# Block sums of w_out formed in DRAM instead of through SBUF, with two moves between queues and engines

## The chip, the cores and the metric

The kernel runs on one core of a Trainium2 chip. The metric is the device time of one execution in microseconds (us), lower is better. The core has five engines that the profile names PE (TensorE, the matrix engine; PEld is its weight load), DVE (VectorE), ACT (ScalarE), POOL (GpSimd) and SP (SyncE, which here only issues transfers). Transfers are issued from SP's, ACT's or POOL's instruction queue and are all carried by the same 16 DMA engines.

## The reference

One layer of an encoder on 512 frames of width 2048, all in float32. Cut to what matters here:

```
h = rmsnorm(x, g_pre);  proj = h @ w_in                # 2048 x 14368+
q, k, v -> conv(4), silu, l2norm;  o_a = gated delta rule, 16 heads, chunks of 64
y_a = (rmsnorm(o_a) * silu(z_a)) @ w_br_a
y_b = (silu(layernorm(conv31(glu(...)))) * silu(z_b)) @ w_br_b
mixed = (gate_a * y_a + gate_b * y_b) @ w_out
x = x + rmsnorm(mixed, g_post)
e = p @ w_ple_proj;  out = x + rmsnorm(sigmoid(x @ w_ple_gate) * e, g_ple)
```

## The kernel before

All large products run on PE as three float32r matmuls each: every operand is split into a high part (a cast on ACT) and a low part (a subtraction, on DVE or POOL), and high x high, high x low and low x high are added in PSUM. The time is a row of such products, one behind the other, and the other engines prepare the next pieces of weights while PE works.

**Start (`load_x`).** PE first makes the embedding `e = p @ w_ple_proj` (`embed`, 4 column tiles x 4 row tiles, 96 matmuls of 128x512). Each result goes from PSUM to an SBUF tile `e_sb` (L233, alternately ACT and DVE) and is stored to `pe_dram` (L309), to be read again at the end. Beside it the four row tiles of x are scaled by their inverse norm: `xss` (ACT and DVE), `xms` (DVE), `xrs` (a power on POOL, L265), then one half of x by DVE (L266) and one by ACT (L267). Then PE transposes x in 16 groups of four 128x128 blocks (`xp`, L313); of each group ACT makes the high part `hh` (L316) and DVE the low part `hl` (L317). The first product with `w_in` (L183, L185, L187: high x high, high weights x low, low weights x high) runs between the transposes. It walks over 16 k-blocks, 4 to a piece of weights. SP loads two pieces in one tile `raw` (L121, 512 KB, three buffers), ACT casts each (`w`, L126), DVE makes its low part (L127), and four `w` buffers stand ready. `hf` and `zsf` (L360) are sums of parts of h for a later stage.

**z, gates (to about 550 us).** A seven-product (Strassen-like) scheme with its block sums of weights on DVE.

**Heads (about 550 to 1490 us).** For 8 groups of two heads PE runs the q, k, v products, and `group` and `head_scan` do the delta rule between them: steps of these generators are taken after so many matmuls (`tick`). Within a group, POOL makes `nk` (L828) and scales `E` (L832); `W` is formed on DVE; its blocks are spread to `Ud` by four copies of 32 partitions x 1024 (L875, all on ACT); DVE transposes `Ud` into `UT` (L881) and solves a triangular system (L892, L893). At a group's end POOL makes `ors` (L786), on which DVE waits for the output of the heads (L790).

**presum.** The last but one product, `mixed @ w_out`, is a seven-product scheme as well. It wants four sums of blocks of w_out: T1 = B11+B12, T3 = B12+B22, T2 = T1+B22, T4 = T2+B21, each as 2 x 4 tiles of 128x1024. `presum` forms them while the heads run, on POOL's queue: blocks are loaded into SBUF tiles `wsum` (L1060, 256 KB), further blocks are added by the transfer itself (`accum_op=add`), and the sums are stored to `wo_sums` (L1065). Per (jp, q) these are 12 loads and 8 stores, 160 transfers in all. They are next read at 2081 us, by L1401.

**Order.** The program is written in one order, and a scheduler then lays each engine's instructions in a fixed order by its own model; `pin` (`keep_in_program_order`) holds instructions it is given. Each engine takes its instructions strictly in that order, so an instruction that waits holds up all behind it on its engine; a transfer waits in the queue of the engine that issues it.

The lines that the prediction speaks of: L309 (stores of the embedding), L265 to L267 (scaling of x), L313 to L317 (transposes), L121, L126, L127 (weights), L183 to L187 (the products), L875 and L881 (`Ud`, `UT`), L786, L828, L832, L847 (POOL's and DVE's steps in a group), L1060 and L1065 (presum).

Of the kernel before, what the change touches and what calls it, by code (L numbers as in the profile page):

```python
# [9 lines left out]
F32 = mybir.dt.float32  # L10
F32R = mybir.dt.float32r
AF = mybir.ActivationFunctionType
ALU = mybir.AluOpType
AX = mybir.AxisListType.X

P = 128
T = 512
# [64 lines left out]
def _body(ctx, tc, A, out):  # L82
    nc = tc.nc
# [7 lines left out]
    slots = ctx.enter_context(tc.tile_pool(name="slots", bufs=21, side="right"))  # L91
# [11 lines left out]
    pin = tc.keep_in_program_order  # L103
# [34 lines left out]
    jobs = deque()  # L138
    active = []

    def spawn(gen, period, key=None):
        active.append([gen, period, period, key])
# [51 lines left out]
    pe_dram = dram.tile([4, NTT, P, T], F32, name="pe_dram")  # L194
# [43 lines left out]
    def load_x():  # L238
        with tc.tile_pool(name="xin", bufs=1) as xin, tc.tile_pool(name="xps", bufs=6, space=PSUM) as xps:
# [66 lines left out]
            nc.sync.dma_start(cst[:, P:], A["consts"][:, P:])  # L306
            nc.sync.dma_start(vec[:, V_DW:], A["vecs"][:, V_DW:])
            for (j, tt), e in e_sb.items():
                nc.sync.dma_start(pe_dram[j, tt], e)  # L309
            for k in range(NK):  # L310
                ps = xps.tile([P, T], F32, tag="xp", name="xp")
                for tt in range(NTT):
# [30 lines left out]
    B11, B12, B22, B21 = range(4)  # L343
# [458 lines left out]
    def group(g):  # L802
# [7 lines left out]
        W = hd.tile([P, 8, 2, 64], F32, tag="W", name="W", bufs=1)  # L810
# [40 lines left out]
        for hh, h, s4, kq, kc, vc in heads:  # L851
            pg = wps.tile([P, NTT, 2, 64], F32, tag="w", name="pg")
            for c in range(8):
                tt, par = divmod(c, 2)
                a = 64 * par
# [12 lines left out]
        U = W[:, :, 0, :]  # L868
        QK = W[:, :, 1, :]

        Ud = hd.tile([P, 32, 4, 8], F32, tag="Ud", name="Ud", bufs=1)
        for qd in range(4):
            r = slice(32 * qd, 32 * qd + 32)
            b = 32 * (qd % 2)
            nc.scalar.copy(Ud[r], U[r, :, b:b + 32].rearrange("p x s -> p s x").unsqueeze(2).broadcast_to([32, 32, 4, 8]))  # L875
        yield
        VT = hd.tile([P, 32, 8], F32, tag="VT", name="VT", bufs=1)
        nc.gpsimd.tensor_copy(VT.rearrange("p j i -> p (j i)"), cc(C_VI, 256))
# [7 lines left out]
        for j in range(30, -1, -1):  # L886
            n, i0 = 32 - j, j // 4
# [161 lines left out]
    WO = A["w_out"]  # L1049
    T1, T2, T3, T4 = range(4)  # L1050
    sums = dram.tile([2, 4, 4, P, 1024], F32, name="wo_sums")
    def presum():
        for jp in range(2):
            for q in range(4):
                cs = [slice(n * T, n * T + T) for n in range(2)]
                a = [slots.tile([P, T], F32, tag="s", name="wsum") for n in range(2)]

                def take(t, blk, add):
                    for n in range(2):
                        nc.gpsimd.dma_start(t[n], WO[jp, blk, q][:, cs[n]], **(dict(accum_op=ALU.add) if add else {}))  # L1060
                        yield

                def give(t, m):
                    for n in range(2):
                        nc.gpsimd.dma_start(sums[jp, m, q][:, cs[n]], t[n])  # L1065
                        yield
                yield from take(a, B11, False)
                b = [slots.tile([P, T], F32, tag="s", name="wsum") for n in range(2)]
                yield from take(b, B12, False)
                yield from take(a, B12, True)  # L1070
                yield from take(b, B22, True)
                yield from give(a, T1)
                yield from give(b, T3)
                yield from take(a, B22, True)
                yield 24
                yield from give(a, T2)
                yield from take(a, B21, True)
                yield 24
                yield from give(a, T4)

    rest = deque([lambda i=i: zb_tile(i) for i in range(FILL, NK)] + [f for i in range(2) for f in (lambda i=i: glu_b(i), lambda i=i: glu_a(i))])
    for g in range(NH // 2):
        pair = (2 * g, 2 * g + 1)
        for h in pair:
            gemm_cm(w_in_tile(16 + h), hT, evac_k(h))
            gemm_cm(w_in_tile(h), hT, evac_q(h))
            gemm_cm(w_in_tile(32 + h), hT, evac_v(h))
        jobs.append(lambda g=g: spawn(group(g), HP, "heads"))
        if g == 0:
            jobs.append(lambda: spawn(presum(), 13, "presum"))  # L1090
        for _ in range(2):
            if rest:
                rest.popleft()()
# [667 lines left out]
```

## Time and profile before

| | |
|---|---|
| median of 3 runs | 2436.09 us (2435.22 to 2436.59) |
| the profiled execution: its own time | 2434.78 us |
| its span, first to last instruction | 2433.0 us |
| PE busy | 2411.8 us, 99% |
| DVE, ACT, POOL busy | 1783.4 (73%), 1210.6 (50%), 491.7 us (20%) |
| moved by DMA | 380 MB, mean 156 GB/s |

The profile has a page (busy time, the chain of waits that ended last, groups of instructions), and views of the trace behind it: who waited for whom, instructions in order of time, busy time by stretch, transfers. Busy time of PE counts matmuls that are pipelined, one beginning before the last has ended, so what PE loses is read as gaps in its order of time. An engine's idle time costs something only where PE stands still for it. The span is 1.8 us shorter than the execution's own time, the rest lying around the first and last instruction.

### The profile page before, as it was taken

How to read it: one execution, taken by the hardware profiler on the slowest of the kernel's cores; microseconds unless marked ns; L12 is line 12 of the kernel's file. 1: busy time of each engine (PE TensorE's matmuls, PEld its weight loads, DVE VectorE, ACT ScalarE, POOL GpSimd, SP SyncE). 2: the span in 40 equal slices, each digit the busy share in tenths (PEclk: the TensorE clock that was granted, in tenths of full speed). 3: DMA queues.
4: the chain of work that ended last, by engine and by line, in shares of the span. 5: the costliest groups of instructions: out<-in, count | busy, mean ns of one | idle time of the engine just before them, and what ended most of it. 6: DMA issues, size and time to landing. Idle time of an engine off the chain costs nothing.

```text
span 2433.0 us, 33728 instructions
## 1 busy us (share of the span) xinstructions
PE 2411.8 (99%) x11966; PEld 1983.7 (82%) x11966; DVE 1783.4 (73%) x3360; ACT 1210.6 (50%) x2355; POOL 491.7 (20%) x521
## 2 busy tenths in 40 slices
PE   9999999999999999999999999999999999999998
PEld 6888888887788888888888887888887888888886
DVE  8877888776677776767777668999988654667644
ACT  6455555555655555564555554454424433554532
POOL 0001110013213031232200001998840000000000
PEclk9999999999999999999999999999999999999999
DMA  7577676757546362657522222443444333665552
GB/s 269 162 200 204 192 208 206 211 155 211 155 140 175 99 187 88 177 149 202 165 89 99 82 80 73 156 139 104 157 133 160 131 130 100 231 223 165 194 175 76
DMA packets 145434, 380.21 MB, mean 156 GB/s; under 512 B 16369, under 2 KB 24817, under 8 KB 145265
## 3 DMA queue, kind: packets, MB, share of 16 engines
q1 hardware_dynamic: 119152, 319.32, 39.3%
q0 software_dynamic: 23808, 54.54, 10.3%
q10 hardware_dynamic: 2304, 4.20, 0.6%
q8 instruction: 94, 1.54, 0.3%
q14 instruction: 76, 0.61, 0.1%
HBM read 329.75 MB, written 48.23 MB: 155 GB/s over the span
## 4 chain that ended last, share of the span: by engine, by line
PE 93%; DVE 4%; ACT 1%; issue 1%; POOL 0%; DMA 0%; SPq 0%; DVEq 0%; POOLq 0%; ACTq 0%
PE g L185 14%; PE g L187 14%; PE g L183 14%; PE zp L473 6%; PE zp L474 6%; PE zp L475 6%; PE yp L1147 4%; PE yp L1145 4%; PE yp L1143 4%; PE f L1438 2%; PE f L1437 2%; PE f L1439 2%; PE f L1610 2%; PE f L1612 2%; PE f L1611 2%; PE psB L760 1%
## 5 line engine op out<-in xcount | busy, mean ns | idle before, releaser
L187 PE MATMUL g<-hh,w 128*128 128x512 f32 x1536 | 609.4, 397 | 3.0 <-DVE w L127 3.0
L185 PE MATMUL g<-hl,w 128*128 128x512 f32 x1536 | 610.4, 397 | 0.0
L183 PE MATMUL g<-hh,w 128*128 128x512 f32 x1536 | 608.5, 396 | 1.0 <-ACT w L126 1.0
L126 ACT CAST w<-raw 128x512 fp32r<-128x512 f32 x580 | 353.2, 618 | 445.6 <-PE g L187 179.6
L127 DVE TENSOR_TENSOR w<-raw,w 128x512 fp32r<-128x512 f32 x466 | 320.8, 695 | 182.0 <-ACT w L126 179.4
L187 PEld LDWEIGHTS g<-hh,w 128*128 128x128 f32 x1536 | 289.0, 188 | 59.8 <-DVE w L127 5.8
L183 PEld LDWEIGHTS g<-hh,w 128*128 128x128 f32 x1536 | 289.2, 188 | 55.5 <-ACT w L126 1.9
L185 PEld LDWEIGHTS g<-hl,w 128*128 128x128 f32 x1536 | 289.0, 188 | 55.5 <-issue 1.2
L1005 DVE SCALAR_TENSOR_TENSOR uc<-up,vec,uc 128x497 f32<-128x497 f32 (+29 forms) x390 | 282.2, 733 | 13.2 <-ACT uc L984 1.9
L127 POOL TENSOR_TENSOR w<-raw,w 128x512 fp32r<-128x512 f32 x114 | 146.9, 1304 | 59.6 <-ACT w L126 59.3
L707 DVE SCALAR_TENSOR_TENSOR cv<-g,vec,cv 128x511 f32<-128x511 f32 x144 | 106.3, 738 | 27.3 <-ACT cv L705 26.6
L1143 PE MATMUL yp<-w,uh 128*128 128x512 f32 x256 | 100.3, 393 | 0.1
L1145 PE MATMUL yp<-w,uh 128*128 128x512 f32 x256 | 100.4, 392 | 0.0
L1147 PE MATMUL yp<-w,ul 128*128 128x512 f32 x256 | 100.4, 392 | 0.0
L1145 PE MATMUL yp<-w,oh 128*128 128x512 f32 x256 | 100.1, 391 | 0.0
L1147 PE MATMUL yp<-w,ol 128*128 128x512 f32 x256 | 99.5, 391 | 0.0
L1143 PE MATMUL yp<-w,oh 128*128 128x512 f32 x256 | 99.1, 389 | 0.0
L892 DVE TENSOR_TENSOR prod<-UT,VT 128x2 f32<-128x2 f32 (+30 forms) x248 | 87.6, 353 | 6.5
L1060 POOL DMA_DIRECT2D wsum<-in_w_out x96 | 75.4, 840 | 66.3 <-DMA wsum<-in_w_out 34.2
L1027 POOL TENSOR_TENSOR uc<-uc,pr 128x511 f32<-128x511 f32 (+29 forms) x60 | 76.2, 1270 | 8.3 <-ACT pr L1026 7.7
L1381 POOL TENSOR_TENSOR rmsm<-totm,mhalf_c 128x2 f32<-128x2 f32 x2 | 2.4, 1202 | 372.6 <-DVE totm L1379 372.6
L1437 PE MATMUL f<-wsp,oph 128*128 128x512 f32 x192 | 75.5, 393 | 0.0
(396 smaller groups left out, 4954.8 us busy)
## 6 DMA issues: line engine op xcount, KB each, us to landing
raw<-in_w_in SPq DMA_DIRECT2D x194, 512.0 KB, 3.3
wsum<-in_w_out POOLq DMA_DIRECT2D x96, 256.0 KB, 5.0
raw<-in_w_ple_gate SPq DMA_DIRECT2D x40, 512.0 KB, 3.3
wo_sums<-wsum POOLq DMA_DIRECT2D x64, 256.0 KB, 3.8
raw<-in_w_br_a SPq DMA_DIRECT2D x32, 512.0 KB, 3.3
raw<-in_w_br_b SPq DMA_DIRECT2D x32, 512.0 KB, 3.3
raw<-in_w_ga SPq DMA_DIRECT2D x24, 512.0 KB, 4.7
raw<-in_w_gb SPq DMA_DIRECT2D x24, 512.0 KB, 4.9
```

What stands on the lines that cost most here:

```text
L126: nc.scalar.copy(hi, rq)
L127: low_part[0].tensor_tensor(lo, rq, hi.bitcast(F32), ALU.subtract)
L183: mm(ps, wh, rh, start=(k == 0), stop=False)
L185: mm(ps, wh, rl, start=False, stop=False)
L187: mm(ps, wl, rh, start=False, stop=(k == NK - 1))
L473: mm(ps[pr][t], lh, wh, start=q + n == 0, stop=False)
L474: mm(ps[pr][t], ll, wh, start=False, stop=False)
L475: mm(ps[pr][t], lh, wl, start=False, stop=q == 3 and n == 1)
L1005: pin(nc.vector.scalar_tensor_tensor(y[:, s:], u[:, 0:T - s], vv(w0 + TAPS - 1 - s), y[:, s:], ALU.mult, ALU.add))
L1143: mm(ps[tt], lh[:, b], wh, start=k == 0, stop=False)
L1145: mm(ps[tt], lh[:, b], wl, start=False, stop=False)
L1147: mm(ps[tt], ll[:, b], wh, start=False, stop=k == NK - 1)
```

## The change

Three things are changed. The 16 stores of the embedding (L309) are issued from POOL's queue instead of SP's. The four `Ud` copies of a group go one to ACT, two to DVE and one to POOL. `presum` no longer passes through SBUF: it copies a block of w_out into the place of the sum in DRAM (16 rows of 32 KB), adds further blocks there by accumulating transfers (128 rows of 4 KB) and copies T1 to T2 and T2 to T4, 64 transfers of 512 KB, one step every 30 ticks instead of 13 and 24. They stay on POOL's queue, and each is given to `pin`.

```diff
--- before.py
+++ after.py
@@ -306,7 +306,7 @@
             nc.sync.dma_start(cst[:, P:], A["consts"][:, P:])
             nc.sync.dma_start(vec[:, V_DW:], A["vecs"][:, V_DW:])
             for (j, tt), e in e_sb.items():
-                nc.sync.dma_start(pe_dram[j, tt], e)
+                nc.gpsimd.dma_start(pe_dram[j, tt], e)
             for k in range(NK):
                 ps = xps.tile([P, T], F32, tag="xp", name="xp")
                 for tt in range(NTT):
@@ -872,7 +872,8 @@
         for qd in range(4):
             r = slice(32 * qd, 32 * qd + 32)
             b = 32 * (qd % 2)
-            nc.scalar.copy(Ud[r], U[r, :, b:b + 32].rearrange("p x s -> p s x").unsqueeze(2).broadcast_to([32, 32, 4, 8]))
+            copy = (nc.scalar.copy, nc.vector.tensor_copy, nc.gpsimd.tensor_copy, nc.vector.tensor_copy)[qd]
+            copy(Ud[r], U[r, :, b:b + 32].rearrange("p x s -> p s x").unsqueeze(2).broadcast_to([32, 32, 4, 8]))
         yield
         VT = hd.tile([P, 32, 8], F32, tag="VT", name="VT", bufs=1)
         nc.gpsimd.tensor_copy(VT.rearrange("p j i -> p (j i)"), cc(C_VI, 256))
@@ -1049,34 +1050,26 @@
     WO = A["w_out"]
     T1, T2, T3, T4 = range(4)
     sums = dram.tile([2, 4, 4, P, 1024], F32, name="wo_sums")
-    def presum():
+    def presum(W, total):
+        def put(jp, m, blk, add=False):
+            how = dict(accum_op=ALU.add, max_dma_last_dim=4096) if add else {}
+            for q in range(4):
+                pin(nc.gpsimd.dma_start(total[jp, m, q], W[jp, blk, q], **how))
+                yield
+
+        def copy(jp, m, n):
+            for q in range(4):
+                pin(nc.gpsimd.dma_start(total[jp, m, q], total[jp, n, q]))
+                yield
         for jp in range(2):
-            for q in range(4):
-                cs = [slice(n * T, n * T + T) for n in range(2)]
-                a = [slots.tile([P, T], F32, tag="s", name="wsum") for n in range(2)]
-
-                def take(t, blk, add):
-                    for n in range(2):
-                        nc.gpsimd.dma_start(t[n], WO[jp, blk, q][:, cs[n]], **(dict(accum_op=ALU.add) if add else {}))
-                        yield
-
-                def give(t, m):
-                    for n in range(2):
-                        nc.gpsimd.dma_start(sums[jp, m, q][:, cs[n]], t[n])
-                        yield
-                yield from take(a, B11, False)
-                b = [slots.tile([P, T], F32, tag="s", name="wsum") for n in range(2)]
-                yield from take(b, B12, False)
-                yield from take(a, B12, True)
-                yield from take(b, B22, True)
-                yield from give(a, T1)
-                yield from give(b, T3)
-                yield from take(a, B22, True)
-                yield 24
-                yield from give(a, T2)
-                yield from take(a, B21, True)
-                yield 24
-                yield from give(a, T4)
+            yield from put(jp, T1, B11)
+            yield from put(jp, T3, B12)
+            yield from put(jp, T1, B12, True)
+            yield from put(jp, T3, B22, True)
+            yield from copy(jp, T2, T1)
+            yield from put(jp, T2, B22, True)
+            yield from copy(jp, T4, T2)
+            yield from put(jp, T4, B21, True)
 
     rest = deque([lambda i=i: zb_tile(i) for i in range(FILL, NK)] + [f for i in range(2) for f in (lambda i=i: glu_b(i), lambda i=i: glu_a(i))])
     for g in range(NH // 2):
@@ -1087,7 +1080,7 @@
             gemm_cm(w_in_tile(32 + h), hT, evac_v(h))
         jobs.append(lambda g=g: spawn(group(g), HP, "heads"))
         if g == 0:
-            jobs.append(lambda: spawn(presum(), 13, "presum"))
+            jobs.append(lambda: spawn(presum(WO, sums), 30, "presum"))
         for _ in range(2):
             if rest:
                 rest.popleft()()
```

The change moves instructions at three places.

DVE at the turn from the embedding to the transposes, before (`x_189` is the last row tile of x, `w` the low parts of weight pieces, `hl` the low parts of h):

```order
28 L266 TENSOR_SCALAR x_189<-x_189,xrs 128x1024
29 L233 COPY e_sb<-e_ps 128x512
30 L127 TENSOR_TENSOR w<-raw,w 128x512
31 L233 COPY e_sb<-e_ps 128x512
32 L127 TENSOR_TENSOR w<-raw,w 128x512
33 L317 SCALAR_TENSOR_TENSOR hl<-xp,vec,hh 128x512 x16
34 L360 TENSOR_TENSOR hf<-hh,hl 128x512 x4
35 L360 TENSOR_TENSOR zsf<-hf 128x256 x2
36 L127 TENSOR_TENSOR w<-raw,w 128x512 x2
```

and changed:

```order
31 L266 TENSOR_SCALAR x_189<-x_189,xrs 128x1024
32 L127 TENSOR_TENSOR w<-raw,w 128x512
33 L233 COPY e_sb<-e_ps 128x512
34 L127 TENSOR_TENSOR w<-raw,w 128x512
35 L317 SCALAR_TENSOR_TENSOR hl<-xp,vec,hh 128x512 x2
36 L127 TENSOR_TENSOR w<-raw,w 128x512
37 L317 SCALAR_TENSOR_TENSOR hl<-xp,vec,hh 128x512
38 L127 TENSOR_TENSOR w<-raw,w 128x512
39 L317 SCALAR_TENSOR_TENSOR hl<-xp,vec,hh 128x512 x6
40 L360 TENSOR_TENSOR hf<-hh,hl 128x512
41 L317 SCALAR_TENSOR_TENSOR hl<-xp,vec,hh 128x512 x6
```

The low parts of the third and fourth weight pieces, which stood behind sixteen `hl`, four `hf` and two `zsf`, now stand behind the second and third `hl`.

POOL at the start, before (`xrs` are the inverse norms of the four row tiles; the row ISA sets POOL up for the power that follows; `zt` belong to the next stage):

```order
6 L99 MEMSET half_c 128x8
7 L101 MEMSET mhalf_c 128x8
8 L265 ISA
9 L265 TENSOR_TENSOR xrs<-xms,mhalf_c 128x1 x4
10 L421 DMA zt<-in_w_z 128x512 x16
```

and changed:

```order
8 L309 DMA pe_dram<-e_sb 128x512 x2
9 L265 ISA
10 L265 TENSOR_TENSOR xrs<-xms,mhalf_c 128x1 x2
11 L309 DMA pe_dram<-e_sb 128x512 x4
12 L265 TENSOR_TENSOR xrs<-xms,mhalf_c 128x1
13 L309 DMA pe_dram<-e_sb 128x512 x6
14 L265 TENSOR_TENSOR xrs<-xms,mhalf_c 128x1
15 L309 DMA pe_dram<-e_sb 128x512 x4
16 L421 DMA zt<-in_w_z 128x512 x16
```

The stores now stand between the four powers, and two of them ahead of the row ISA.

POOL from the end of the second group of heads into the third, before (`ors` ends a group, `nk` and `E` begin the next):

```order
69 L718 COPY kq<-kc 128x4x2x64
70 L786 TENSOR_TENSOR ors_7778<-ors,mhalf_c 128x4
71 L786 TENSOR_TENSOR ors_7782<-ors,mhalf_c 128x4
72 L828 TENSOR_TENSOR nk<-sk,half_c 128x4
73 L832 TENSOR_TENSOR E<-E,c_all 128x256
74 L828 TENSOR_TENSOR nk<-sk,half_c 128x4
75 L832 TENSOR_TENSOR E<-E,c_all 128x256
76 L1060 DMA wsum<-in_w_out 128x512 x8
```

and changed (an L1062 row is a copy of a sum to the next sum, 16x8192, an L1057 row with 128x1024 an addition):

```order
65 L786 TENSOR_TENSOR ors_7740<-ors,mhalf_c 128x4
66 L786 TENSOR_TENSOR ors_7744<-ors,mhalf_c 128x4
67 L1062 DMA wo_sums<-wo_sums 16x8192
68 L1057 DMA wo_sums<-in_w_out 128x1024
69 L828 TENSOR_TENSOR nk<-sk,half_c 128x4
70 L832 TENSOR_TENSOR E<-E,c_all 128x256
71 L1062 DMA wo_sums<-wo_sums 16x8192
72 L828 TENSOR_TENSOR nk<-sk,half_c 128x4
73 L832 TENSOR_TENSOR E<-E,c_all 128x256
74 L1062 DMA wo_sums<-wo_sums 16x8192
75 L1057 DMA wo_sums<-in_w_out 128x1024
76 L876 COPY Ud<-W 32x1024
```

Transfers that add to what a transfer just ahead of them copies now stand between POOL's steps of a group, and the copy of `Ud` behind them. PE's own order is the same in both programs except among the transposes at the start.

## Rows read from the trace of the kernel before

**Rows 1.** The page: busy time of each engine, and the chain that ended last.
```profile
PE 2411.8 (99%) x11966; PEld 1983.7 (82%) x11966; DVE 1783.4 (73%) x3360; ACT 1210.6 (50%) x2355; POOL 491.7 (20%) x521
...
PE 93%; DVE 4%; ACT 1%; issue 1%; POOL 0%; DMA 0%; SPq 0%; DVEq 0%; POOLq 0%; ACTq 0%
```

**Rows 2.** Busy time by stretch: stretch, length, PE, PEld, DVE, ACT, POOL, clock, DMA, GB/s.
```profile
0.00:60.00 60.00, 54.21 (x250) 41.80 (x251) 49.20 (x90) 39.22 (x65) 2.89 (x10) 1.00 0.73 269
...
200.00:300.00 100.00, 100.00 (x443) 82.77 (x442) 80.41 (x129) 51.00 (x86) 10.71 (x12) 1.00 0.73 204
...
600.00:700.00 100.00, 98.41 (x546) 79.50 (x545) 71.72 (x157) 60.17 (x107) 25.39 (x33) 1.00 0.58 171
```

**Rows 3.** Whom PE waited for, whole span: us in total, times, longest.
```profile
PE g L187 <- DVE w L127: 3.0, 2, 2.5
```

**Rows 4.** SP's queue in order of time, 19 to 50 us.
```profile
19.22 13.36 SPq L309 DMA_DIRECT2D pe_dram<-e_sb  x16
32.63 16.49 SPq L121 DMA_DIRECT2D raw<-in_w_in  x5
```

**Rows 5.** DVE in order of time, 32 to 47 us.
```profile
32.06 10.62 DVE L317 SCALAR_TENSOR_TENSOR hl<-xp,vec,hh 128x512 fp32r<-128x512 f32 x16
42.59 2.48 DVE L360 TENSOR_TENSOR hf<-hh,hl 128x512 f32<-128x512 f32 x4
...
45.67 1.28 DVE L127 TENSOR_TENSOR w<-raw,w 128x512 fp32r<-128x512 f32 x2
```

**Rows 6.** PE in order of time, 23 to 47 us: start, us, engine, line, [idle before].
```profile
23.92 0.39 PE L228 MATMUL e_ps<-w,ph 128*128 128x512 f32 x1
...
29.43 2.83 PE L313 MATMUL xp<-cst,x 128*128 128x128 f32 x24
...
43.53 0.39 PE L185 MATMUL g<-hl,w 128*128 128x512 f32 x1
46.41 0.50 PE L187 MATMUL g<-hh,w 128*128 128x512 f32 x1 [2.48 <-DVE w L127]
```

**Rows 7.** Transfers of raw, 0 to 60 us, issue to landing.
```profile
DMA to landing us min/median/max: 3.1/5.7/10.0
```

**Rows 8.** POOL in order of time: the first power, and four transfers issued later.
```profile
12.54 0.88 POOL L265 TENSOR_TENSOR xrs<-xms,mhalf_c 128x1 f32<-128x1 f32 x1 [11.66 <-DVE xms L263]
...
22.01 0.55 POOL L265 TENSOR_TENSOR xrs<-xms,mhalf_c 128x1 f32<-128x1 f32 x1 [4.92 <-DVE xms L263]
...
653.25 2.33 POOL L1060 DMA_DIRECT2D wsum<-in_w_out  x4
```

**Rows 9.** ACT's steps on x and on the projection's weights at the start.
```profile
17.65 1.15 ACT L267 ACTIVATE x<-x,xrs 128x1024 f32<-128x1024 f32 x1
...
20.22 1.13 ACT L279 CAST w<-raw 128x512 fp32r<-128x512 f32 x2
```

**Rows 10.** ACT, DVE and PE in order of time around the first group's Ud.
```profile
648.80 8.14 ACT L875 COPY Ud<-W 32x1024 f32<-32x1024 f32 x4
...
656.97 1.25 DVE L881 STREAM_TRANSPOSE UT<-Ud 128x1024 f32<-128x1024 f32 x1 [8.22 <-ACT Ud L875]
...
657.63 0.50 PE L183 MATMUL g<-hh,w 128*128 128x512 f32 x1 [0.98 <-ACT w L126]
658.84 0.50 PE L187 MATMUL g<-hh,w 128*128 128x512 f32 x1 [0.48 <-DVE w L127]
```

**Rows 11.** POOL's copies of 128x512, line L718: ns min, median, max.
```profile
L718 POOL COPY kq<-kc x16: 607/656/1122, 581.3 to 1362.2; 128x512 f32<-128x512 f32 x16
```

**Rows 12.** POOL and DVE in order of time, second group's end, third group.
```profile
845.95 1.01 POOL L786 TENSOR_TENSOR ors<-ors,mhalf_c 128x4 f32<-128x4 f32 x1 [1.99 <-DVE ors L784]
...
859.73 0.69 DVE L847 TENSOR_TENSOR vh<-pv,nk 128x512 f32<-128x512 f32 x1 [0.68 <-PE pv L844]
...
872.14 1.25 DVE L881 STREAM_TRANSPOSE UT<-Ud 128x1024 f32<-128x1024 f32 x1 [6.86 <-ACT Ud L875]
```

**Rows 13.** Transfers that touch wsum (256 KB), whole span, issue to landing.
```profile
DMA to landing us min/median/max: 2.3/4.8/10.1
```

## The prediction

> **What bounds the kernel.** I read the page first: PE is busy 99% of the span and makes 93% of the chain that ended last, POOL 0% [rows 1]. So nothing that the change does on POOL, DVE, ACT or the DMA engines counts unless PE stands still for it. Busy time by stretch then shows where PE does stand still: 60 - 54.21 = 5.8 us in the first 60 us and 1.6 us between 600 and 700 [rows 2], of 2433.0 - 2411.8 = 21.2 us in the whole span [rows 1]. The steady rate is 443 matmuls of 128x512 in 100 us, 0.226 us each at the full granted clock [rows 2], and no edit touches their number. The last product and what follows it are left alone. What can be won is therefore a few us: the list of whom PE waited for names two waits for the low part of weights (3.0 us, the longest 2.5) [rows 3], the order of time one for a cast (0.98) [rows 10], and these are the waits that two of the three edits reach.
>
> **The stores of the embedding, from SP to POOL.** SP issued the 16 stores from 19.22 on, for 13.36 us, because the later ones wait for copies of the embedding; the second tile of w_in stood behind them and was issued at 32.63 [rows 4]. The scheduler knew that and put that tile's low parts on DVE behind all sixteen `hl`, four `hf` and two `zsf`, at 45.67 [rows 5]. PE had begun its last matmul at 43.53 (it ended its turn at 43.53 + 0.23 = 43.76) and went on at 46.41 [rows 6]: 2.65 us lost. Before that, from 29.43 to 43.76, PE did 64 transposes at 2.83/24 = 0.118 us and 26 matmuls at 0.226 us [rows 2, 6], 7.55 + 5.88 = 13.43 us of work in 14.33, so 0.9 us more were lost among the transposes. In the changed order the two low parts stand behind the second and third `hl`. Does DVE keep up? It does an `hl` in 10.62/16 = 0.66 us, an `hf` in 0.62, a low part in 0.64 [rows 5]; if it starts `hl` at 32.06 as now, the last `hl` is done at 32.06 + 10.62 + 2 x 0.64 + 2 x 0.62 = 45.2 and the fifth low part, behind one more `hf` (0.62) and itself (0.64), at 46.5. PE without a gap wants the last `hl` after 45 matmuls, at 29.43 + 7.55 + 45 x 0.226 = 47.2, and the fifth piece after 48, at 47.8 [rows 2, 6]. DVE is ahead by 1.3 to 2 us, so the stall goes. The tile must land by about 33; SP is free for it at 19.22 [rows 4], and a raw tile took at most 10.0 us to land in this stretch [rows 7]. The gain lies between 0 (the tile or DVE late after all) and 2.65 + 0.9 = 3.55 us; I take **2.7**, the whole stall and next to nothing of the 0.9, because `hl` starts no earlier.
>
> On POOL the stores are 16 issues. Four back to back took 2.33 us, 0.58 each [rows 8]; they now stand around the four powers. A power that comes late holds ACT's scaling of the first two tiles of x, and behind these stand the casts of the fourth projection tile, which PE wants at 23.92 [rows 6]. The first power now stands behind the second store, which needs the second copy of the embedding. That copy ends before 12.54, when the first power ran [rows 8], so with the 0.58 of its issue the power moves to 13.1 at most, by 0.6 us. From the power to the cast are 0.9 + 2 x 1.15 + 0.57 = 3.8 us [rows 8, 9], 16.9 against 23.92: no cost, with 7.0 us to spare. The third and fourth power stand behind 4 and 6 stores, 2.3 and 3.5 us of issue, in which POOL had 4.92 us of idle time [rows 8]. What is unknown is what the row ISA costs, which has moved behind two stores. Before, it was hidden: POOL sat idle 11.66 us ahead of the first power, and the only sign is that the first power took 0.88 us and the third 0.55 [rows 8]. So its bounds are 0.3 and 11.7 us; I take 0.3, the row that shows it, and price the upper end as a rival below.
>
> The Trainium skill, GPSIMD Engine Reference, section 2.1 (Instruction dispatch), states that the first call to a freshly loaded GpSimd kernel pays about 6 us for loading its code, with no instruction visible in the profile, and this speaks against putting stores ahead of the row ISA. By that figure the estimate is that the first power ends near 20.0 and the sum stays as it is with about 1 us to spare; the trace neither shows nor excludes it.
>
> **The copies of Ud.** In the first group ACT spent 8.14 us on four copies, DVE waited 8.22 us for them, and the casts and low parts behind them came so late that PE lost 0.98 and 0.48 us, 1.46 in all [rows 10]. Now ACT does one (2.03 us) and is free 6.1 us earlier. DVE does two, between 1.25 (its own pass over 1024 elements) and 2.03 each; POOL one, between 2 x 0.61 = 1.2 and 2 x 1.12 = 2.2 us [rows 10, 11]. DVE goes on after at most 4.1 us instead of 8.22. Both waits of PE go: **1.46**; at worst 0. In the other groups DVE waited about as long (6.86 in the third [rows 12]) and PE lost nothing, so nothing is won there.
>
> **presum.** 160 transfers become 64, and with the 16 stores POOL issues 80 instead of 160, at 0.58 us some 46 us less of issue, on an engine that is not on the chain [rows 1, 8]. I cost it at 0. The cover is POOL's slack within a group: what its waits could hold up is the slow rival. For the weight loads on SP: a tile lasts PE 24 x 0.226 = 5.4 us and three buffers stand, so a load may land 10.8 us after its issue before a cast is late; with the DMA engines at 0.73 the longest took 10.0 [rows 2, 7], and in this stage their share is 0.58 [rows 2].
>
> **The sum.** 2.7 + 1.46 = 4.2 us off the profiled execution's span of 2433.0, so 2428.8, and off its own time of 2434.78, so 2430.6. The median of the runs lies 1.3 above that execution: 2436.1 - 4.2 = **2431.9**. Nothing later gives it back: PE's order is the same behind the start, and the heads' steps are counted in matmuls.
>
> **Rivals.**
> *All of the start is won.* The 0.9 among the transposes goes too, because low parts of weights let PE fill its gaps, and the embedding's own small gaps shrink (part of the 5.8 - 2.65 - 0.9 = 2.3 us left in the first 60 us [rows 2]; some 0.3). Then 3.55 + 0.3 + 1.46 = 5.3, 2430.8. For it: PE has matmuls ready from the second `hl` on. Against: nothing starts the transposes earlier than 29.43.
>
> *The start is not won.* Either the row ISA takes long, or the second raw tile comes no earlier. For the first, the point is 7.0 us from row ISA to first power; beyond it PE waits us for us, at the bound of 11.7 this costs 11.7 - 7.0 = 4.7 and eats everything: 2436.6. For the second, the stall of 2.65 stays: 2434.6. It spans 2433 to 2436.6. The Trainium skill, DMA: Bandwidth & Descriptors, section Issuing engines are not separate DMA queues, says that spreading transfers over engines only saves issue time, which is usually small. By that rule the term would be near 0; here the trace shows 13.36 us in which SP was held [rows 4], and that is what is saved.
>
> *POOL waits for DRAM* (the slower one). In the third and fifth groups a copy and an addition to its result stand between `ors` and `nk`, and in the fifth again ahead of `Ud`; the addition holds POOL until the copy has landed. `ors` ends at 846.96; `vh` wants the second `nk` by 859.73, and from POOL's release to that are two powers (as long as `ors`, 1.01 each), an `E` (0.61) and an issue (0.58): released by 856.5, so the copy may take 9 us; DVE may then be held about 6.9 more, as it is now without a loss [rows 12], which makes 16; ahead of `Ud`, by the same count, 11. A 256 KB transfer landed in 2.3 to 10.1 us [rows 13]; twice the bytes give 2.3 to 20.2. I take about 6, from the median of 4.8. At 15 the loss equals the gain; at 20.2 it is 2 x 4.2 + 9.5 = 18, and the time 2450. Against: PE lost nothing to POOL's waits for presum before.
>
> **Chances.** Forecast (2431.2 to 2432.9) 0.46; all of the start 0.30; start not won 0.16; POOL waits 0.08. A measurement of this kernel tells about 0.2% (4.9 us, below 2431.2 or above 2441) from no change: faster 0.30, same 0.46 + 0.16 = 0.62, slower 0.08. The range reaches from 2430.4, the whole start with the spread of the runs, to 2436.6, the start not won; only the slow rival and the ends lie outside.
>
> **What would show it.** Right: no wait of PE near 46 us and none near 657; raw's second tile issued near 19 us; DVE's wait for `Ud` at 2 to 4 us; the busy share of 0 to 60 us up by about 2.7. Wrong: PE waiting at 24 us or at the first transposes (the powers late), low parts of w_in still late on DVE, POOL held for more than 9 us ahead of `nk`, or PE waiting at new places between 650 and 1200 us. If PE's gaps shrink as said and the time does not, something later takes it back, and the theory is wrong.

## The result, and the profile after

The changed kernel took 2430.21 us in the median of 9 runs (2428.67 to 2433.04), the kernel before 2436.09 (2435.02 to 2437.74) beside it: a ratio of 0.9977, with a 95% interval of 0.9968 to 0.9986. That is 5.9 us less, where 4.2 were forecast; the interval reaches from 3.4 to 7.8 us.

The profiled execution of the changed kernel is the slowest of the nine, 2433.04 us with a span of 2431.3. This matters, since one stage of it is not typical. A second profile of the same kernel was taken later (called the second profile here): its own time is 2428.72 us, its span 2426.9. First the page of the first profile, engines and chain, against [rows 1].

```profile
PE 2411.2 (99%) x11966; PEld 1985.0 (82%) x11966; DVE 1811.8 (75%) x3376; ACT 1163.3 (48%) x2331; POOL 449.8 (19%) x449
PE 92%; DVE 4%; DMA 2%; issue 1%; ACT 1%; POOL 0%; SPq 0%; DVEq 0%; POOLq 0%; ACTq 0%
```

PE's work is the same. POOL has 42 us less to do, ACT 47 us less, DVE 28 us more. New in the chain are 2% of DMA. The waits of PE (us in total, times, longest), against [rows 3], say where:

```profile
PE xp L313 <- DVE hl L317: 3.6, 1, 3.6
```

Both waits of PE for the low part of weights are gone, and so is the one for a cast; a wait of 3.6 us among the transposes has come. Here is that place in order of time, for PE and DVE:

```profile
37.29 0.66 PE L313 MATMUL xp<-cst,x 128*128 128x128 f32 x4 [3.62 <-DVE hl L317]
...
30.62 1.40 DVE L317 SCALAR_TENSOR_TENSOR hl<-xp,vec,hh 128x512 fp32r<-128x512 f32 x2
35.88 0.69 DVE L127 TENSOR_TENSOR w<-raw,w 128x512 fp32r<-128x512 f32 x1 [3.86 <-ACT w L126]
```

What the transfers of `raw` took from issue to landing between 10 and 46 us:

```profile
DMA to landing us min/median/max: 3.9/11.9/14.6
```

SP's queue and ACT, again in order of time, show the rest of the chain: the tile is issued 12 us earlier than before [rows 4], but ACT still waits for it until 35.23.

```profile
20.59 17.59 SPq L121 DMA_DIRECT2D raw<-in_w_in  x4
...
35.23 0.62 ACT L126 CAST w<-raw 128x512 fp32r<-128x512 f32 x1 [4.08 <-DMA raw<-in_w_in]
```

So the tile was on its way for 14.6 us (20.59 + 14.6 = 35.2), and two `hl` further on DVE stood behind it. The second profile has the same stall, smaller: the tile landed after at most 13.4 us, ACT cast it at 33.30, and PE waited 2.03 us. PE in order of time, and then the landing:

```profile
35.36 0.66 PE L313 MATMUL xp<-cst,x 128*128 128x128 f32 x4 [2.03 <-DVE hl L317]
```
```profile
DMA to landing us min/median/max: 4.5/11.9/13.4
```

Busy time by stretch (stretch, length, then PE, PEld, DVE, ACT, POOL, granted clock, DMA share, GB/s) shows that the 1.6 us between the two waits is not the whole difference. First profile:

```profile
30.00:34.00 4.00, 3.67 (x27) 2.89 (x25) 2.02 (x4) 1.15 (x2) 1.09 (x2) 1.00 1.02 413
34.00:38.00 4.00, 0.71 (x5) 0.69 (x6) 2.12 (x4) 2.77 (x6) 0.00 (x0) 1.00 0.92 376
38.00:42.00 4.00, 4.00 (x17) 3.16 (x16) 4.00 (x7) 2.42 (x5) 0.00 (x0) 0.60 0.45 150
```

Second profile:

```profile
34.00:38.00 4.00, 2.64 (x18) 2.13 (x18) 4.00 (x7) 4.00 (x8) 0.00 (x0) 1.00 1.03 415
38.00:42.00 4.00, 4.00 (x31) 3.49 (x29) 4.00 (x7) 3.37 (x7) 0.00 (x0) 1.00 0.28 110
```

The 16 DMA engines are full or nearly so up to about 38 us in both (shares of 0.92 to 1.03). Behind the gap of 3.6 us the clock granted to PE was 0.60 in the mean of 4 us, so for most of them the lower of its two levels, 1.2 instead of 2.4 GHz, in which PE did 17 instructions; behind the gap of 2.0 us it stayed at full speed, and PE did 31.

Two marks cut the span into parts that can be compared between kernels, since PE's order is the same behind the transposes: the start of the matmul `sw_ps` (L666, just behind the z stage) and PE's first listed wait for the output of the heads (`po`, L794). Kernel before, changed kernel, and its second profile, in this order:

```profile
580.29 0.43 PE L666 MATMUL sw_ps<-ba_s,cst 128*128 128x64 f32 x2 [0.64 <-ACT ba_s L662]
1489.18 0.59 PE L794 MATMUL po<-cst,O 128*128 128x128 f32 x2 [0.76 <-DVE O L790]
```
```profile
582.21 0.43 PE L666 MATMUL sw_ps<-ba_s,cst 128*128 128x64 f32 x2 [0.60 <-ACT ba_s L662]
1487.39 0.59 PE L794 MATMUL po<-cst,O 128*128 128x128 f32 x2 [0.76 <-DVE O L790]
```
```profile
577.97 0.43 PE L666 MATMUL sw_ps<-ba_s,cst 128*128 128x64 f32 x2 [0.60 <-ACT ba_s L662]
1483.13 0.59 PE L794 MATMUL po<-cst,O 128*128 128x128 f32 x2 [0.80 <-DVE O L790]
```

The heads (from mark to mark) took 908.89 us before and 905.18 and 905.16 after: 3.7 us less in both, to 0.02 us. What is ahead of the first mark took 1.9 us more in the first profile and 2.3 us less in the second. What is behind the second mark takes 943.8 to 943.9 us in all three. So the heads give 3.7 us in both profiles.

The start has to be read more closely, because PE's first transpose already comes 0.7 and 1.1 us earlier than in the kernel before (29.43 [rows 6]), and three profiles below in which nothing ahead of it was changed have it 0.4 to 0.7 us earlier as well. So I count from the first transpose to the matmul that stood behind the stall of before (the L187 at 46.41 [rows 6]): 16.98 us before. First profile, then second:

```profile
28.69 3.38 PE L313 MATMUL xp<-cst,x 128*128 128x128 f32 x28
...
47.46 0.39 PE L187 MATMUL g<-hh,w 128*128 128x512 f32 x1
```
```profile
28.35 3.37 PE L313 MATMUL xp<-cst,x 128*128 128x128 f32 x28
...
43.90 0.39 PE L187 MATMUL g<-hh,w 128*128 128x512 f32 x1
```

That is 18.77 and 15.55 us: 1.8 us lost in the first profile and 1.4 won in the second, and the landing of one tile decides which. (In four profiles below with the stores on SP as before, the same count gives 16.97 to 17.01.)

Where the 3.7 come from is seen at the fifth group. Before, ACT made its four copies of `Ud` until 1087.65 and only then cast the next weights, and PE's matmuls, otherwise 0.227 us apart, came 0.34 to 0.41 apart. ACT and PE before:

```profile
1079.47 8.18 ACT L875 COPY Ud<-W 32x1024 f32<-32x1024 f32 x4 [1.75 <-DVE W L861]
...
1088.29 2.18 ACT L126 CAST w<-raw 128x512 fp32r<-128x512 f32 x4
...
1088.55 0.39 PE L187 MATMUL g<-hh,w 128*128 128x512 f32 x1
1088.96 0.50 PE L183 MATMUL g<-hh,w 128*128 128x512 f32 x1
1089.30 0.40 PE L185 MATMUL g<-hl,w 128*128 128x512 f32 x1
1089.69 0.50 PE L187 MATMUL g<-hh,w 128*128 128x512 f32 x1
1090.03 0.39 PE L183 MATMUL g<-hh,w 128*128 128x512 f32 x1
```

ACT and PE after, where the cast comes 7.7 us earlier:

```profile
1078.21 2.02 ACT L876 COPY Ud<-W 32x1024 f32<-32x1024 f32 x1 [2.68 <-DVE W L861]
...
1080.62 0.60 ACT L126 CAST w<-raw 128x512 fp32r<-128x512 f32 x1
...
1087.69 0.39 PE L187 MATMUL g<-hh,w 128*128 128x512 f32 x1
1087.92 0.39 PE L183 MATMUL g<-hh,w 128*128 128x512 f32 x1
```

From 1088.55 to 1090.03 there are four steps, 1.48 us where 0.91 would do: 0.57 us lost, in pieces too small for the list of waits. Matching PE's instructions one by one between the two kernels shows where the 3.7 us lie: 2.3 in the first group, 0.6 in this one, and 0.1 to 0.2 in most of the others.

### The profile page after: what moved, and what is told of

Read it like the earlier page. It is cut to its first block, busy times and chain, and to the rows that moved or that the text cites. A ratio compares the mean times of both kernels' runs of the same rounds, so it can differ in the third digit from the quotient of the medians.

```text
span 2431.3 us, 33577 instructions
## 1 busy us (share of the span) xinstructions
PE 2411.2 (99%) x11966; PEld 1985.0 (82%) x11966; DVE 1811.8 (75%) x3376; ACT 1163.3 (48%) x2331; POOL 449.8 (19%) x449
## 4 chain that ended last, share of the span: by engine, by line
PE 92%; DVE 4%; DMA 2%; issue 1%; ACT 1%; POOL 0%; SPq 0%; DVEq 0%; POOLq 0%; ACTq 0%
PE g L185 14%; PE g L187 14%; PE g L183 14%; PE zp L475 6%; PE zp L473 6%; PE zp L474 6%; PE yp L1140 4%; PE yp L1138 4%; PE yp L1136 4%; PE f L1431 2%; PE f L1432 2%; PE f L1430 2%; PE f L1605 2%; PE f L1603 2%; PE f L1604 2%; PE psB L760 1%
## 5 line engine op out<-in xcount | busy, mean ns | idle before, releaser
L187 PE MATMUL g<-hh,w 128*128 128x512 f32 x1536 | 609.0, 397 | 0.0
L187 PEld LDWEIGHTS g<-hh,w 128*128 128x128 f32 x1536 | 289.3, 188 | 53.9 <-POOL w L127 0.3
L718 POOL COPY kq<-kc 128x512 f32<-128x512 f32 x16 | 11.5, 721 | 383.9 <-ACT kc L716 225.5
L1603 PE MATMUL f<-w,xh 128*128 128x512 f32 x192 | 75.5, 393 | 0.0
```

The source lines that it names most:

```text
L187: mm(ps, wl, rh, start=False, stop=(k == NK - 1))
```

## The experiments

All were timed against the kernel before on the same chip. "Start" is the time of the first mark, "heads" that from mark to mark, in each run's profile. A start is that of one execution, and it carries up to 1.1 us either way from ahead of the first transpose, which no edit explains; the profile of the kernel with held stores is the slowest of its five runs.

| kernel | median us | ratio (95% interval) | start | heads |
|---|---|---|---|---|
| before | 2436.1 to 2436.4 | 1 | 580.29 | 908.89 |
| changed | 2430.21 | 0.9977 (0.9968 to 0.9986) | 582.21 | 905.18 |
| changed, again | 2429.54 | 0.9974 (0.9963 to 0.9985) | 577.97 | 905.16 |
| stores on POOL alone | 2435.71 | 0.9997 (0.9988 to 1.0006) | 581.15 | 909.04 |
| Ud copies spread alone | 2439.46 | 1.0012 (1.0003 to 1.0021) | 579.85 | 912.44 |
| sums in DRAM alone | 2435.05 | 0.9996 (0.9987 to 1.0005) | 580.04 | 908.35 |
| changed, stores on SP | 2431.94 | 0.9980 (0.9972 to 0.9989) | 579.60 | 905.15 |
| before, Ud on ACT and DVE | 2432.32 | 0.9985 (0.9976 to 0.9994) | 581.91 | 905.81 |
| changed, stores held | 2427.67 | 0.9963 (0.9949 to 0.9977) | 579.09 | 905.13 |
| changed, held, tile early | 2428.28 | 0.9965 (0.9953 to 0.9978) | 577.21 | 905.17 |
| changed, tile early | 2427.48 | 0.9964 (0.9952 to 0.9977) | 577.14 | 905.13 |
| changed, tile early, stores on SP | 2429.10 | 0.9972 (0.9961 to 0.9982) | 578.21 | 905.16 |
| before, held, Ud on ACT and DVE | 2428.16 | 0.9967 (0.9955 to 0.9979) | 577.99 | 905.22 |

**The three edits, each alone.** The first theory was that they simply add. Stores on POOL alone:

```diff
-                nc.sync.dma_start(pe_dram[j, tt], e)
+                nc.gpsimd.dma_start(pe_dram[j, tt], e)
```

> The kernel before with the embedding's stores on POOL alone. Theory: the start gains what the changed kernel's other runs show and its profiled one lost, about 2 us in the median (2434), with a wider spread than before (4 to 5 us between runs), because the second tile of w_in now competes with the stores; in its profile the wait at 46 us is gone and, in a late case, one of 1 to 4 us stands among the transposes. Rival: the stores on POOL gain nothing (2435.5 to 2436.5) and the whole gain of the change lies in the heads.

Measured 2435.71, with runs from 2432.53 to 2437.34: 0.5 us in the median and a spread of 4.8, so the median goes with the rival and the spread with the theory. Its profile is a late case: the tile landed after 14.6 us, PE waited 2.7 us among the transposes, and from the first transpose to the L187 it took 0.7 us more than before. So alone this edit gives nothing that is clear of noise.

Copies of `Ud` alone:

```diff
-            nc.scalar.copy(Ud[r], ...)
+            copy = (nc.scalar.copy, nc.vector.tensor_copy, nc.gpsimd.tensor_copy, nc.vector.tensor_copy)[qd]
+            copy(Ud[r], ...)
```

> The kernel before with the four copies of Ud spread alone. Theory: all that PE gained between 580 and 1490 us in the changed kernel, 3.6 us, comes from this edit, so 2432.5, with no small gaps at the casts of the later groups. Rival: only the two waits at 657 us go (1.46 us, 2434.6) and the other 2 us come from the sums in DRAM.

Measured 2439.46, slower than before; neither theory nor rival had this. The profile names the place. POOL in order of time in the fifth group, with the sums through SBUF as before:

```profile
1082.83 0.57 POOL L1066 DMA_DIRECT2D wo_sums<-wsum  x1 [2.71 <-DMA wsum<-in_w_out]
1084.13 0.91 POOL L1061 DMA_DIRECT2D wsum<-in_w_out  x1 [0.72 <-DMA wo_sums<-wsum]
1085.55 0.89 POOL L1061 DMA_DIRECT2D wsum<-in_w_out  x1 [0.51 <-DMA wo_sums<-wsum]
1086.48 1.90 POOL L876 COPY Ud<-W 32x1024 f32<-32x1024 f32 x1
```

DVE and PE of the same stretch, and then busy time by stretch:

```profile
1088.42 1.25 DVE L882 STREAM_TRANSPOSE UT<-Ud 128x1024 f32<-128x1024 f32 x1 [9.53 <-POOL Ud L876]
...
1090.29 0.80 PE L187 MATMUL g<-hh,w 128*128 128x512 f32 x1 [4.07 <-DVE w L127]
```
```profile
1086.00:1092.00 6.00, 1.93 (x5) 1.42 (x5) 3.34 (x11) 0.47 (x1) 3.98 (x5) 0.77 0.87 170
1092.00:1098.00 6.00, 6.00 (x19) 4.69 (x19) 5.38 (x24) 1.10 (x2) 0.90 (x1) 0.67 0.86 246
```

POOL's copy stood in its queue behind loads and stores of the sums, each of which waited for a transfer; DVE had begun its own two copies at 1076.53 and 1077.79 and then waited 9.53 us, PE 4.07, and behind that gap the granted clock was 0.77 and 0.67 in two stretches. The first four groups had gained 2.7 us by then (matched instruction by instruction), and this one place cost 6.4.

Sums in DRAM alone:

> The kernel before with the sums formed in DRAM alone. Theory: nothing, 2435.5 to 2436.5, since POOL and the DMA engines are off the chain and PE's two waits at 657 us stay. Rival: it gains 2 us in the later groups of heads (2434). A third case: it loses where POOL's additions wait for copies ahead of nk (over 2437).

The diff is the third part of the change. Measured 2435.05, and the heads 0.5 us shorter in the profile: nothing that is clear of its interval, as the theory had it.

**The two edits of the heads together**, the changed kernel with L309 back on `nc.sync`:

> The changed kernel with the stores of the embedding back on SP: the copies of Ud and the sums in DRAM together. Theory: 2432.5, as the copies alone, with the wait of 2.5 us at 46 us back and a spread between runs as narrow as before. If the two edits of the heads help or hinder each other, it lies off the sum of the two alone by more than 1 us.

Measured 2431.94. Alone they gave +3.2 and -1.2 us, together -4.3: they help each other by about 6 us. The expected 2432.5 was nearly met, but not because the copies alone are worth it; the last sentence of the expectation is the one that held. To see whether the sums in DRAM are needed, or only POOL must be out of the way, the copies went to ACT and DVE in turn, in the kernel before:

```diff
-            nc.scalar.copy(Ud[r], ...)
+            copy = (nc.scalar.copy, nc.vector.tensor_copy, nc.scalar.copy, nc.vector.tensor_copy)[qd]
+            copy(Ud[r], ...)
```

> The kernel before with the copies of Ud on ACT and DVE in turn, none on POOL, and the sums still through SBUF. Theory: what made the spread copies alone slow was POOL's copy behind the sums' transfers in the fifth group; without POOL the waits at 657 us and the small ones of the later groups go and nothing new comes, so 2432 to 2433. Rival: the sums through SBUF themselves stand against a faster turn of the heads (their transfers collide with the weights); then a wait of PE near 1086 us comes here too and the time stays over 2436.

Measured 2432.32, and no wait of PE in the fifth group: POOL's place in line was the fault, and the sums in DRAM are worth next to nothing where POOL has no copy to make. (Its heads are 0.7 us longer than those of the changed kernel. The difference is one step of 0.92 instead of 0.24 us near 637 us, where PE waits for a step on DVE (`E_mk`, L689); the last kernel below has the same copies and not that wait.) In the changed kernel POOL's queue in the same group shows how near it is:

```profile
1061.06 0.58 POOL L1062 DMA_DIRECT2D wo_sums<-wo_sums  x1
1066.40 0.84 POOL L1057 DMA_DIRECT2D wo_sums<-in_w_out  x1 [4.75 <-DMA wo_sums<-wo_sums]
...
1071.82 0.60 POOL L1062 DMA_DIRECT2D wo_sums<-wo_sums  x1
1076.32 0.87 POOL L1057 DMA_DIRECT2D wo_sums<-in_w_out  x1 [3.90 <-DMA wo_sums<-wo_sums]
1078.24 2.01 POOL L876 COPY Ud<-W 32x1024 f32<-32x1024 f32 x1 [1.06 <-DVE W L861]
```

Two additions wait there for their copies, 4.75 and 3.90 us, and POOL is at the copy of `Ud` 1.06 us before its data.

POOL's copy has another price. The 16 copies of `Ud` on DVE, in ns (least, median, most), in the changed kernel and then in the kernel with none on POOL:

```profile
L876 DVE COPY Ud<-W x16: 1080/1858/2678, 650.7 to 1403.5; 32x1024 f32<-32x1024 f32 x16
```
```profile
L876 DVE COPY Ud<-W x16: 1071/1082/1093, 651.0 to 1402.2; 32x1024 f32<-32x1024 f32 x16
```

In every group the DVE copy that begins beside POOL's takes 2.6 to 2.7 us, the second one 1.1; with POOL idle, or late as in the fifth group of the copies alone (1.06), both take 1.1. So POOL relieves ACT of a copy of 2.0 us and costs DVE 1.6, and the heads come out the same either way (905.2 us).

**The start.** First the changed kernel once more:

> The changed kernel as it is, for a second profile and more times. Theory: 2430 to 2431, with runs from 2428.5 to 2433, wider than those of the kernel with the stores on SP (2429.8 to 2432.8); the second tile of w_in, issued near 20.6 us beside the stores, lands between 30 and 35 us, and the later it lands, the longer the wait of PE among the transposes. Rival: the spread comes from elsewhere, and the landing is the same in a fast profile as in the slow one.

Measured 2429.54 (2428.49 to 2433.66), with the profile shown above: the tile landed 1.9 us sooner than in the first, PE waited 1.6 us less for it, and the first mark came 4.2 us sooner. The mechanism of the theory held; the median came in 0.5 us under its range. Then the stores were held behind the four powers on POOL, by giving both to `pin`:

```diff
-                nc.gpsimd.tensor_tensor(rs, ms, mhalf_c[:, 0:1], ALU.pow)
+                pin(nc.gpsimd.tensor_tensor(rs, ms, mhalf_c[:, 0:1], ALU.pow))
...
-                nc.gpsimd.dma_start(pe_dram[j, tt], e)
+                pin(nc.gpsimd.dma_start(pe_dram[j, tt], e))
```

> The changed kernel with the four powers and the sixteen stores held in the order of the program on POOL, so that all stores start behind the last power, near 28 us. Theory: the second tile of w_in then has the DMA engines with little beside it, lands before 29 us, PE waits neither among the transposes nor at 46 us, and the time is 2428 to 2429.5 with a narrow spread. Rival: the tile's landing is set by what SP loads before it (x, constants, vectors), not by the stores; then it still lands late and the time stays at 2430 to 2431.

Measured 2427.67 (2427.23 to 2430.09), slightly under the range, and the spread is not as narrow as expected. POOL's stores in order of time, and then the landing of `raw` between 10 and 46 us:

```profile
29.11 6.96 POOL L309 DMA_DIRECT2D pe_dram<-e_sb  x12
```
```profile
DMA to landing us min/median/max: 3.3/6.4/8.1
```

At most 8.1 us instead of 14.6, and no wait of PE at the transposes beyond the 0.6 that the kernel before has there. From the first transpose to the L187 PE takes 14.37 us, 2.6 less than before. It was the stores beside it that made the tile late, not SP's loads ahead of it. With the tile also issued ahead of the late constants:

```diff
             prep()
+            prep()
             nc.sync.dma_start(cst[:, P:], A["consts"][:, P:])
```

> As the kernel with the held stores, and SP issues the second tile of w_in ahead of the late parts of the constants and vectors. Theory: the tile lands some 2 us earlier still, but nothing waits for it any more, so the same time as with held stores alone, within 0.5 us. Rival: if the tile was late behind the constants, this one gains 1 to 3 us over held stores alone.

Measured 2428.28, the same within the intervals, as the theory said. The same line without the held stores:

> The changed kernel with SP issuing the second tile of w_in ahead of the late parts of the constants and vectors, stores on POOL where the scheduler puts them (4 and 6 of them between the powers). The tile is issued near 17 us instead of 20.6. Theory: if a landing takes as long as in the changed kernel (12 to 14.6 us), it comes at 29 to 31 us; DVE now wants it ahead of its first low part of h, at about 30.5, so PE waits 0 to 1 us, and the time is 2427.5 to 2429.5. Rival: with the stores in the queues the tile lands after 32 us, everything behind it is late, and the time is 2430 or more.

Measured 2427.48 (2426.66 to 2428.76), the lowest median of all, though not clear of the two kernels with held stores. A landing still takes long in this stretch, but the tile starts early enough that ACT finds it there (the landing of `raw`, and then ACT in order of time):

```profile
DMA to landing us min/median/max: 3.9/9.8/12.9
```
```profile
30.14 1.13 ACT L126 CAST w<-raw 128x512 fp32r<-128x512 f32 x2
```

Is POOL needed for that at all? With that line and the stores on SP:

> The stores stay on SP, and SP issues the second tile of w_in ahead of the late constants and so ahead of all stores; the copies of Ud and the sums in DRAM as changed. Theory: what was won at the start was this tile's place in line, not the engine of the stores, so this reaches the same 2427.5 to 2429, with the third tile now behind the stores, issued near 33 us, in time. Rival: SP held by the stores makes the third tile late (PE waits near 50 us) and the gain shrinks to 2430 or more.

Measured 2429.10, between the two cases. At the transposes PE is as well off as with held stores and the tile early (14.85 us to the L187, against 14.88), and up to 100 us the two profiles stay together; the start is 1.0 us later (578.21 against 577.21), in two places of the z stage, near 105 and 127 us, of which the list of waits has 0.2 us, a wait of PE for a block sum on DVE. Such steps are in the first profile of the changed kernel too (0.9 us) and in that of the sums in DRAM alone (0.5), which has the stores and the third tile as before, so the later third tile need not be the cause, and it stays open. So of the 4.5 us between the medians of the stores on SP (2431.94) and the lowest, 2.8 are won by the tile's place in line alone. Last, the two findings in the kernel before, without the sums in DRAM: stores held on POOL, `Ud` on ACT and DVE.

> The kernel before with the stores held behind the powers on POOL and the copies of Ud on ACT and DVE in turn, the sums still through SBUF in 160 transfers. Theory: nothing of the gain comes from forming the sums in DRAM, once POOL has no copy of Ud to make; so 2428 to 2429, as the changed kernel with held stores. Rival: the sums in DRAM are worth 1 us or more by themselves; then 2429.5 or more.

Measured 2428.16, and heads of 905.22 us with all 160 transfers through SBUF. The sums in DRAM give nothing of their own that can be measured here.

## Why the prediction was right, and where its steps were wrong

**The time.** 2431.9 was forecast, in a range from 2430.4 to 2436.6. The median is 2430.21, a little under that range, and the measured ratio, applied to the median of before, gives 2430.5 (2428.3 to 2432.7). The sign and the size were right; the make-up of the sum was not. The heads gave 3.7 us where 1.46 were forecast, and the stores, where the scheduler put them, gave nothing that is clear of noise where 2.7 were forecast. That the two errors pull against each other, so that the total comes out near, is luck. By its time the outcome lies nearest to the rival in which all of the start is won (2430.8), but it did not come about in that way.

**The stores.** The stall at 46 us went, as the forecast said: PE's L187 behind it has no wait. The failed step is that the tile "must land by about 33", for which it was taken that "a raw tile took at most 10.0 us to land in this stretch" [rows 7]. That row was of a program in which SP issued the stores one by one ahead of the tile. With the stores on POOL the tile goes beside them, and took 13.4 and 14.6 us. Nor was 33 early enough: in the second profile the tile landed near 33.2, and PE still waited 2.03 us, because the changed order has low parts of the tile behind the second `hl`, which DVE had done by 32. The rival "the second raw tile comes no earlier" was in the list as half of a case of 0.16, priced at 2.65 us; in the first profile it cost more, since the clock fell behind the gap. The term of 2.7 us measured 1.4 in the second profile and -1.8 in the first, from the first transpose to the matmul behind the stall of before. In the medians, the changed kernel against the one with its stores on SP, it is 1.7 us, or 2.4 by the second set of runs, but only 0.7 and 1.5 by the ratios, whose intervals overlap widely (0.9968 to 0.9986 and 0.9963 to 0.9985, against 0.9972 to 0.9989). The size forecast was right of what there was to win: where the tile is not late, with held stores or with the tile early, the same count gives 2.1 to 2.9 us.

**The rule on queues.** The Trainium skill, DMA: Bandwidth & Descriptors, section Issuing engines are not separate DMA queues, says that another issuing engine saves only issue time. The prediction set against it that SP was held for 13.36 us [rows 4]. Both were half right here: the tile was issued 12 us earlier (20.59 instead of 32.63), and the DMA engines, full as they were (a share of 1.02), took 14.6 us for it. What is won by an earlier issue has to be read at the landing.

**The powers.** The row ISA was priced at 0.3 us, with 7.0 to spare. POOL in the first profile:

```profile
12.10 0.57 POOL L309 DMA_DIRECT2D pe_dram<-e_sb  x1 [0.68 <-DVE xms L263]
12.77 0.92 POOL L265 TENSOR_TENSOR xrs<-xms,mhalf_c 128x1 f32<-128x1 f32 x1
```

The second store's issue ends at 12.67 and the first power begins at 12.77. It came 0.23 us later than before [rows 8], against 0.6 allowed, and no engine noticed. The 6 us of the Trainium skill, GPSIMD Engine Reference, section 2.1, do not show here: 0.10 us is all the room there is between the issue and the power.

**The copies of Ud.** Forecast 1.46 us, measured 3.7. DVE went on 3.9 us after its first copy began (650.65 to 654.52), against at most 4.1 forecast and 8.22 us of waiting before [rows 10]; 3.7 of them were its own two copies, 2.6 and 1.1 us, where between 1.25 and 2.03 each had been allowed, and POOL's took 2.0, within its bounds. PE's two waits there went, as said, but they were mis-sized: a gap is listed from the modelled end of a matmul, 0.39 us behind its start, while the next could have begun after 0.227. Counted from start to start the two cost 1.14 and 0.64 us instead of 0.98 and 0.48, and with small steps beside them the first group gave 2.3. The failed step is that in the other groups "PE lost nothing, so nothing is won there": the list of waits leaves out steps of 0.34 us, and the spacing of the matmuls shows them, 1.4 us over the other groups, 0.6 of it in the fifth. It could have been read before: 0.34 instead of 0.227 us between starts, behind the late casts of the first six groups.

**presum.** "I cost it at 0" is right of the edit alone (ratio 0.9996) and wrong of its part in the whole. The forecast priced POOL's copy of `Ud` at its own 1.2 to 2.2 us and looked for POOL's waits only in the new form of the sums; with the transfers of before in POOL's queue that copy once began 8.7 us behind DVE's second (1086.48 against 1077.79), and the edit that wins 3.7 us lost 3.2. The sums in DRAM paid for that.

**The slow rival.** POOL waiting for DRAM ahead of `nk` and `Ud` was named, with a landing of about 6 us for a copy, 11 as the point from which it costs ahead of `Ud`, and 15 as that at which the gain is gone. The copies took 5.3 and 4.5 us in the fifth group (issue and wait), and `Ud` had 1.06 us to spare. It did not happen; that its other form, through SBUF, costs 6.4 us at the same place was seen only when the edits were taken apart.

## What to carry to other kernels

Before work is moved onto an idle engine, read that engine's queue and not its busy share: an instruction that waits for a transfer holds up all compute behind it, and an engine at 20% can still be nine microseconds late. Look also at what runs beside it: a copy on DVE took 2.7 us beside one on POOL and 1.1 without. An earlier issue is worth what the landing says: where the DMA engines are full, first move the transfer that something waits for ahead of those that nothing waits for. And for an engine that is busy 99%, compare the spacing of its instructions with their best spacing; the listed waits leave out what is lost in tenths of a microsecond.

## What was not expected of the hardware

A gap on PE can cost more than its length. Behind gaps of 3.62 and 4.07 us the granted clock fell to 0.60 (38 to 42 us, changed kernel) and 0.77 and 0.67 (1086 to 1098 us, copies alone), and in the second case 12 matmuls came 0.43 us apart instead of 0.227, 12 x 0.2 = 2.4 us more. Behind a gap of 2.5 us it went both ways: the kernel before kept 1.00 (44 to 52 us), while in the kernel with `Ud` on ACT and DVE, at the same gap of 2.50 us at 46.46, the rows are

```profile
44.00:48.00 4.00, 1.54 (x4) 1.25 (x5) 4.00 (x8) 1.66 (x3) 0.00 (x0) 0.82 0.01 2
48.00:52.00 4.00, 4.00 (x15) 3.17 (x14) 2.19 (x6) 1.34 (x3) 0.00 (x0) 0.75 0.81 261
```

and its start is 1.6 us later than that of the kernel before for that alone: matched one by one, PE's instructions come 0.05 us later than in the kernel before ahead of that stretch, and 1.62 later behind it. This may widen the runs of kernels with a gap near that length at the start, but it is not shown. Without such a gap, the runs with held stores and the tile early lie within 1.1 us (2427.59 to 2428.64) and those with held stores alone within 2.9 (2427.23 to 2430.09); those of the changed kernel itself lie within 4.4 (2428.67 to 2433.04). The share of the clock in that spread was not measured run by run.
